# Stick-breaking attention of a prompt on one core: one-pass products for the logits, and merged suffix sums

## Chip, core and metric

The kernel runs on one core of a Trainium2 chip. The metric is the device time of one execution in microseconds (us). Engines are named as in the profile: PE is TensorE (matmuls), PEld its weight loads, DVE VectorE, ACT ScalarE, POOL GpSimd, SP SyncE, whose queue issues most DMAs. L2153 is line 2153 of the kernel before.

## The reference

One inference step of a two-layer decoder, for a prompt of 512 tokens and for 8 samples of 4 new tokens each, in f32. Layer 0 mixes tokens with a conformer convolution, layer 1 with stick-breaking attention (16 heads of 64 channels); each is followed by a gated FFN. What matters here is the attention of the prompt:

```python
z = jnp.einsum('bqhd,bkhd->bhqk', q, k) * (HEAD_DIM ** -0.5)
z = z + bias[None, :, None, None]
valid = k_pos[None, :] < q_pos[:, None]
log_fail = jnp.where(valid, jax.nn.log_sigmoid(-z), 0.0)
after = lax.cumsum(log_fail, axis=3, reverse=True) - log_fail
weights = jnp.where(valid, jnp.exp(jax.nn.log_sigmoid(z) + after), 0.0)
out = jnp.einsum('bhqk,bkhd->bqhd', weights, v)
```

For each query the weight of a key is a product of a sigmoid and of (1 - sigmoid) of all later keys before the query. With s = softplus(z) the logarithm of the weight is z minus the sum of s over this and all later keys. The samples attend to 256 cached tokens in pages of 128, and to their own new ones.

## The kernel before

**Arithmetic.** Most products are made of high and low parts. A value x is split into hi, x rounded to the type F32R, and lo = x - hi; a product is then three one-pass matmuls, hi with hi, hi with lo, lo with hi. A matmul with plain f32 operands takes the PE four passes, and shows in the trace as two instructions.

**Stages.** Layer 0, then in layer 1 the queries, then the keys (with the logits of the samples against the K pages in between), then one stage for the values, the attention of the prompt and the V pages of the samples, then the output projection, the FFN and the final norm. The change touches the third stage of layer 1, 746 to 919 us of the profiled execution.

**A planned stage.** Its instructions are not issued in program order. `Plan` (L75) collects operations, each with its engine, an estimated cost and what it reads and writes (`r`, `w`, and `a` for adding into a PSUM bank). `run` (L154) then gives each engine one fixed order by simulating these costs: of the operations that are ready it takes the one that can start first, with an advantage in proportion to its rank, the length of the longest chain behind it. On the chip each engine runs its order and waits on semaphores. `plan.tile` (L145) makes rings of buffers: a tile waits until the users of the one that many turns before are done.

**What the stage does.** For each chunk c of 128 channels, that is for each pair of heads, in this order of emission:

- `values` (L2024): V of the next chunk, as three-pass products (L2018 to L2020), and its transposition into `vtok` (L2046 to L2051), which goes to memory too.
- `page` (L2087): two of the 16 V pages of the samples. POOL gathers a page by an indirect DMA (L2094) into a ring of `PAGE_BUFS` = 3 buffers, PE multiplies it (L2105), and DVE or ACT adds the result into `oacc`.
- `pair` (L2142): the attention of the two heads j = 0 and 1, which lie on rows 0 to 63 and 64 to 127 of `qT` and `kT`.

`logits` (L2146) computes z transposed, keys on partitions and queries along the columns, so that a key chunk needs only the queries behind it. There are three groups of PSUM banks, two banks each: `zc` holds key chunk 3 against queries 384 to 511 (K3, 128 columns) and key chunk 2 against queries 256 to 511 (K2, 256 columns); `zb` holds key chunk 1 (384 columns); `za` key chunk 0 (512 columns). A bf16 product of the identity with `maskb2` then adds a large negative number where key and query conflict (L2156).

`softplus` (L2163) gives s in `spc`, `spb`, `spa` by exp, min, ln and max on ACT and DVE by turns. `parts_of` (L2172) makes the high part on POOL (`ha`, `hb`, `hc`) and the low part on DVE (`la`, `lb`, `lc`). `minus` (L2178) then subtracts suffix sums in PSUM by matmuls with constant weights: `ntri` is the triangle of -1 within a chunk, `nones` all -1 for whole later chunks; `ntri_r` and `nones_r` are the same in F32R. For `zc`, chunk 3 goes through f32 `ntri` and `nones` (L2205, L2206) and only chunk 2 and the sum of both chunks (columns 384 to 511 of `spc`, L2203) through parts. Last, ACT takes exp into `wc`, `wb` and `spa`, and `products` (L2231) multiplies the weights with `vtok`; the result replaces the queries in `qT` (L2240) and is split into `XH` and `XL` (L2261, L2262) for the output projection, whose first four groups (`begun`, L2266) belong to the same plan.

**Around it.** After the queries, `xT` (the residual) is saved to memory (L1716) and its place serves as page buffers `page_t` and for `wT`; L2257 loads it back on SP's queue before L2289 adds the output projection to it. `decode_weights` (L2061) turns the samples' logits `Zd`, `Zn` into weights `wT` and `wn` by a suffix sum of many DVE steps (L1891), at the start of the stage. `new_values` (L2119) adds the samples' own tokens into `oacc` and transposes it (L2132). The constants `nones`, `ntri`, `maskf`, `maskb` are made at the start of the kernel (L355 to L367), and their F32R and doubled forms at the start of the stage (L1974 to L1980).

Of the kernel before, what the change touches and what calls it, by code (L numbers as in the profile page):

```python
# [195 lines left out]
def tile_trunk(  # L196
# [84 lines left out]
    class Ring:  # L281
# [60 lines left out]
        def free(self, later=None):  # L342
# [16 lines left out]
    pool.affine_select(out=ntri, in_=ntri, compare_op=ALU.is_ge, fill=0.0, base=0,  # L359
                       pattern=[[-1, P]], channel_multiplier=1)  # L360
    maskf = base.tile([P, P], F32, name="maskf")
    pool.memset(maskf, 0.0)

    pool.affine_select(out=maskf, in_=maskf, compare_op=ALU.is_gt, fill=NEG, base=0,
                       pattern=[[1, P]], channel_multiplier=-1)
    maskb = base.tile([P, P], BF16, name="maskb")
    dve.tensor_copy(maskb, maskf)  # L367
    eps_t = base.tile([P, 1], F32, name="eps_t")
# [1402 lines left out]
    Zd = dz.tile([P, 4, KW], F32, name="Zd")  # L1771
    Zn = dz.tile([P, 4, NS], F32, name="Zn")
    Sn = dz.tile([P, 4, NS], F32, name="Sn")
    nsn = dz.tile([P, 4], F32, name="nsn")
# [192 lines left out]
    plan = Plan()  # L1967
    vw_cm, vw = open_pool("vw", side="right")
# [3 lines left out]
    wn = va.tile([P, 4, P], F32, name="wn")  # L1972
    oacc = vw.tile([P, 2, 2 * P], F32, name="oacc")
    nones_r = va.tile([P, P], F32R, name="nones_r")  # L1974
    dve.tensor_copy(nones_r, nones)
    ntri_r = va.tile([P, P], F32R, name="ntri_r")
    dve.tensor_copy(ntri_r, ntri)
    maskb2 = va.tile([P, 2, P], BF16, name="maskb2")
    for i in range(2):
        pool.tensor_copy(maskb2[:, i, :], maskb)  # L1980
    pool.memset(vtok_s, 0.0)
# [14 lines left out]
    def acost(n):  # L1996
        return 0.1 + n * 0.95e-3
# [144 lines left out]
    def pair(c):  # L2142
        zs = {}
        K3, K2 = (0, 3, 3 * P), (P, 2, 2 * P)

        def logits(tag, parts, mask):  # L2146

            z = zs[tag] = [psum(tag) for _ in range(2)]

            def f():  # L2150
                for i, (lo, kc, q0) in enumerate(parts):
                    for j in range(2):
                        pe.matmul(z[j]()[:, lo:lo + SEQ - q0], kT[HALF[j], c, kc * P:(kc + 1) * P], qT[HALF[j], c, q0:SEQ],  # L2153
                                  start=(i == 0), stop=False, skip_group_check=True)
                for j in range(2):
                    pe.matmul(z[j]()[:, 0:mask], identb, maskb2.rearrange("p i q -> p (i q)")[:, :mask],  # L2156
                              start=False, stop=True, skip_group_check=True)
# [24 lines left out]
        def sums(t):  # L2182
            return t.rearrange("p (a q) -> p a q", q=P)[:, 0:3:2, :]

# [7 lines left out]
        for j in range(2):  # L2192
            h = 2 * c + j
            b = bb[:, h:h + 1]
            spa, spb, spc = sbuf("spa", 512, 3), sbuf("spb", 384, 2), sbuf("spc", 512, 2)
            ha, hb, hc = sbuf("ha", 512, 1, F32R), sbuf("hb", 384, 2, F32R), sbuf("hc", 384, 2, F32R)
            la, lb, lc = sbuf("la", 512, 1, F32R), sbuf("lb", 384, 2, F32R), sbuf("lc", 384, 2, F32R)
            wb, wc = sbuf("wb", 384, 2), sbuf("wc", 384, 2)
            z3, z1, z0 = zc[j], zb[j], za[j]
# [10 lines left out]
            plan.op("act", acost(384), lambda wc=wc, z3=z3, b=b: act.activation(wc(), z3()[:, :384], AF.Exp, bias=b),  # L2210
                    r=[z3], w=[wc])
# [5 lines left out]
            plan.op("act", acost(384), lambda wb=wb, z1=z1, b=b: act.activation(wb(), z1()[:, :384], AF.Exp, bias=b),  # L2217
                    r=[z1], w=[wb])
            for x in (hb, lb):
# [8 lines left out]
            heads.append({3: (wc, slice(0, P)), 2: (wc, slice(P, 384)), 1: (wb, slice(0, 384)), 0: (spa, slice(0, 512))})  # L2228
        av = psum("one")
# [18 lines left out]
    for c in range(NC):  # L2248
# [7 lines left out]
        pair(c)  # L2256
    plan.op("sp", 3.0, lambda: nc.sync.dma_start(out=xflat, in_=xsave), w=["pages"] + [("wT", t) for t in range(4)])  # L2257
    plan.op("sp", 3.0, lambda: nc.sync.dma_start(out=vsv, in_=vtok_s[:NS, :]), r=[("vnew", i) for i in range(NC)])
# [22 lines left out]
    close(vw_cm)  # L2281
    close(vt_cm)
# [51 lines left out]
```

## Time and profile before

| | us |
|---|---|
| median of 3 runs | 1355.88 |
| lowest and highest | 1354.37, 1357.83 |
| the profiled execution, its own time | 1356.08 |
| span of its profile, first to last instruction | 1354.4 |
| stage of values and attention, within the span | 746 to 919 |

The profile's page gives busy time and share of the span for each engine, then the chain of work that ended last. A window row gives for one stretch the busy time of each engine, with the granted TensorE clock as a share of full speed. A timeline row has the start, the time until the last of the merged instructions ended, engine, line, operation, output and inputs, and their number; in brackets the idle time before it and what ended it. Matmuls overlap in the pipeline, so how long one takes is read from start to start. Grouped rows have the count, the busy time in us, the mean in ns and the idle time before.

### The profile page before, as it was taken

What the parts mean: (1) busy time and instruction counts of PE and PEld (TensorE: products, weight loads), DVE (VectorE), ACT (ScalarE), POOL (GpSimd) and SP (SyncE); (2) the same over time, 40 slices, a digit from 0 to 9 for tenths busy, and PEclk for the clock granted to TensorE, in tenths of its full rate; (3) what the DMA queues carried; (4) which work ended last, traced back from release to release, by engine and by line L of the source; (5) the groups of instructions that cost most, each with busy time, mean ns of one, the idle gap of its engine ahead of it and who ended that gap; (6) DMA issues with size and microseconds to landing.
All of it is one profiled execution on the core that took longest, in us unless ns stands there. A gap on an engine that the chain in (4) does not pass through costs nothing.

```text
span 1354.4 us, 26784 instructions
## 1 busy us (share of the span) xinstructions
PE 1318.0 (97%) x11018; PEld 1242.8 (92%) x11018; DVE 975.6 (72%) x1650; ACT 668.9 (49%) x1242; POOL 240.5 (18%) x379
## 2 busy tenths in 40 slices
PE   8999999999999999998999999999899999999997
PEld 7897799899999999998999777769899999999997
DVE  5599785878987877856253776663897896786762
ACT  6421574545554554544333566753654654454452
POOL 3201014301010010033221242222520010000012
PEclk9899999999999999999999999999999999999998
DMA  8273523123233233235365242322122233233221
GB/s 227 67 185 103 126 95 109 32 86 102 87 111 101 73 111 114 76 118 181 126 205 166 80 129 90 102 94 63 63 79 83 92 110 110 75 100 109 86 73 66
DMA packets 124492, 142.39 MB, mean 105 GB/s; under 512 B 5672, under 2 KB 117992, under 8 KB 124099
## 3 DMA queue, kind: packets, MB, share of 16 engines
q1 hardware_dynamic: 118003, 122.43, 29.4%
q0 software_dynamic: 6080, 18.25, 4.3%
q8 instruction: 86, 1.41, 0.4%
q14 instruction: 35, 0.29, 0.1%
q10 hardware_dynamic: 288, 0.02, 0.0%
HBM read 129.34 MB, written 12.18 MB: 104 GB/s over the span
## 4 chain that ended last, share of the span: by engine, by line
PE 84%; DVE 9%; ACT 3%; issue 1%; DMA 1%; POOL 0%; SPq 0%; DVEq 0%; ACTq 0%; POOLq 0%
PE acc L1441 5%; PE acc L1439 5%; PE acc L1440 5%; PE acc L425 4%; PE acc L426 4%; PE acc L427 4%; PE tr L1252 4%; PE tr L1251 4%; PE tr L1253 3%; PE av L1251 3%; PE av L1252 3%; PE av L1253 3%; PE acc L651 3%; PE acc L653 3%; PE acc L652 3%; PE tr L1441 3%
## 5 line engine op out<-in xcount | busy, mean ns | idle before, releaser
L328 DVE TENSOR_TENSOR wlo<-raw,whi 128x1024 fp32r<-128x1024 f32 (+2 forms) x244 | 258.5, 1064 | 77.5 <-ACT whi L325 77.1
L325 ACT CAST whi<-raw 128x1024 fp32r<-128x1024 f32 (+2 forms) x244 | 223.0, 916 | 153.5 <-PE tr L1252 30.5
L651 PE MATMUL acc<-XH,whi 128*128 128x288 f32 (+1 forms) x384 | 114.9, 299 | 0.0
L653 PE MATMUL acc<-XH,wlo 128*128 128x288 f32 (+1 forms) x384 | 111.0, 289 | 1.8 <-DVE wlo L328 1.8
L652 PE MATMUL acc<-XL,whi 128*128 128x288 f32 (+1 forms) x384 | 111.3, 290 | 0.0
L425 PE MATMUL acc<-XH,whi 128*128 128x288 f32 (+1 forms) x360 | 107.8, 300 | 0.6 <-DVE xT L1598 0.6
L426 PE MATMUL acc<-XL,whi 128*128 128x288 f32 (+1 forms) x360 | 104.0, 289 | 0.0
L427 PE MATMUL acc<-XH,wlo 128*128 128x288 f32 (+1 forms) x360 | 103.6, 288 | 0.0
L1441 PE MATMUL acc<-TH,wlo 128*128 128x272 f32 x288 | 83.4, 290 | 0.0
L1439 PE MATMUL acc<-TH,whi 128*128 128x272 f32 x288 | 83.2, 289 | 0.0
L1440 PE MATMUL acc<-TL,whi 128*128 128x272 f32 x288 | 83.1, 288 | 0.0
L1475 ACT COPY G<-acc 128x272 f32<-128x272 f32 (+1 forms) x72 | 26.9, 373 | 110.3 <-PE acc L1441 95.4
L651 PEld LDWEIGHTS acc<-XH,whi 128*128 128x128 f32 x384 | 72.7, 189 | 2.7 <-issue 2.1
L653 PEld LDWEIGHTS acc<-XH,wlo 128*128 128x128 f32 x384 | 72.8, 190 | 2.2 <-DVE wlo L328 2.2
L1252 PE MATMUL av<-HL,whi 128*128 128x288 f32 (+1 forms) x256 | 74.4, 290 | 0.0
L1251 PE MATMUL av<-HH,whi 128*128 128x288 f32 (+1 forms) x256 | 74.3, 290 | 0.0
L1253 PE MATMUL av<-HH,wlo 128*128 128x288 f32 (+1 forms) x256 | 74.0, 289 | 0.0
L1251 PE MATMUL tr<-HH,whi 128*128 128x256 f32 (+1 forms) x256 | 73.6, 288 | 0.0
L1252 PE MATMUL tr<-HL,whi 128*128 128x256 f32 (+1 forms) x256 | 73.4, 287 | 0.0
L652 PEld LDWEIGHTS acc<-XL,whi 128*128 128x128 f32 x384 | 72.8, 190 | 0.5
L1253 PE MATMUL tr<-HH,wlo 128*128 128x256 f32 (+1 forms) x256 | 73.0, 285 | 0.0
L1393 DVE SCALAR_TENSOR_TENSOR cv<-G,fprm,cv 128x560 f32<-128x560 f32 x88 | 69.9, 798 | 4.2 <-ACT cv L1390 3.0
(461 smaller groups left out, 4456.0 us busy)
## 6 DMA issues: line engine op xcount, KB each, us to landing
raw<-in_ffn_w_gate_dram SPq DMA_DIRECT2D x22, 1024.0 KB
raw<-in_ffn_w_up_dram SPq DMA_DIRECT2D x22, 1024.0 KB
raw<-in_ffn_w_down_dram SPq DMA_DIRECT2D x24, 768.0 KB
raw<-in_attn_w_qkv_dram SPq DMA_DIRECT2D x12, 1024.0 KB
raw<-in_conv_w_in_dram SPq DMA_DIRECT2D x6, 1024.0 KB
rep<-glu SPq DMA_DIRECT2D x36, 142.0 KB
raw<-in_conv_w_out_dram SPq DMA_DIRECT2D x4, 1024.0 KB
raw<-in_ffn_w_down_dram SPq DMA_DIRECT2D x8, 512.0 KB
```

Source lines behind the costliest of these rows:

```text
L325: act.copy(hi[:, :n, :], src)
L328: dve.tensor_tensor(lo[:, :n, :], src, hi[:, :n, :], op=ALU.subtract)
L425: pe.matmul(o, hi[:, k, :], xh[:, k, c0:c0 + n], start=(k == 0), stop=False)
L426: pe.matmul(o, hi[:, k, :], xl[:, k, c0:c0 + n], start=False, stop=False)
L427: pe.matmul(o, lo[:, k, :], xh[:, k, c0:c0 + n], start=False, stop=(k == nk - 1))
L651: pe.matmul(o, hi[:, k, :], XH[:, k, c0:c0 + n], start=(k == 0), stop=False)
L652: pe.matmul(o, hi[:, k, :], XL[:, k, c0:c0 + n], start=False, stop=False)
L653: pe.matmul(o, lo[:, k, :], XH[:, k, c0:c0 + n], start=False, stop=(k == NC - 1))
L1251: pe.matmul(o, hi[:, j + k, :], xh, start=(start and k == 0), stop=False, **kw)
L1252: pe.matmul(o, hi[:, j + k, :], xl, start=False, stop=False, **kw)
L1253: pe.matmul(o, lo[:, j + k, :], xh, start=False, stop=(stop and k == len(xs) - 1), **kw)
L1441: pe.matmul(o, lo[:, j + k, :], xh, start=False, stop=(k == 3), **kw)
```

## The change

Four things change.

1. **Logits.** Before a pair's logits, POOL copies the chunk of `qT` and of `kT` to F32R (`qh`, `kh`) and DVE subtracts (`ql`, `kl`), 512 columns each, in rings of one buffer. Each f32 product becomes three products of parts.
2. **Sums.** `hc` and `lc` are the parts of all 512 columns of `spc`. One `ntri_r` product of 384 columns for each part covers chunks 3 and 2, and one `nones_r` product of 128 columns takes chunk 3 off chunk 2; the f32 ones go.
3. **Weights in place.** The exponentials overwrite `spc` and `spb`, which become rings of three; `wc` and `wb` go.
4. **Places.** The constants are made on POOL after the queries, in the pools of the samples' attention. `Zn` and `Sn` move into the unused end of `xT`'s place. `wn` and `oacc` move into the third page buffer, so that V pages go through a ring of two, one page fewer is gathered ahead in the stage of the keys, and the reload of `xT` waits for `Zn`, `oacc` and `wn` as well.

```diff
-    nones = base.tile([P, P], F32, name="nones")
-    dve.memset(nones, -1.0)
-    ntri = base.tile([P, P], F32, name="ntri")
-    pool.memset(ntri, -1.0)
...
+    nones = small.tile([P, P], F32, name="nones")
+    pool.memset(nones, -1.0)
+    nones_r = dz.tile([P, P], F32R, name="nones_r")
+    pool.tensor_copy(nones_r, nones)
+    ntri_r = dz.tile([P, P], F32R, name="ntri_r")
+    pool.affine_select(out=nones, in_=nones, compare_op=ALU.is_ge, fill=0.0, base=0,
+                       pattern=[[-1, P]], channel_multiplier=1)
+    pool.tensor_copy(ntri_r, nones)
+    maskf = small.tile([P, P], F32, name="maskf")
+    pool.memset(maskf, 0.0)
+    pool.affine_select(out=maskf, in_=maskf, compare_op=ALU.is_gt, fill=NEG, base=0,
+                       pattern=[[1, P]], channel_multiplier=-1)
+    maskb2 = dz.tile([P, 2, P], BF16, name="maskb2")
+    for i in range(2):
+        pool.tensor_copy(maskb2[:, i, :], maskf)
...
-        if i >= 4 * NB:
+        if i >= 2 * NB + PAGE_BUFS - 1:
...
+    spare = page_t[(2 * NB - 1) % PAGE_BUFS]
+    wn = spare[:, 0:4 * P].rearrange("p (t r) -> p t r", t=4)
+    oacc = spare[:, 4 * P:].rearrange("p (g r) -> p g r", g=2)
...
-        t = plan.tile("page", PAGE_BUFS, lambda: page_t[(2 * NB + p) % PAGE_BUFS])
+        t = plan.tile("page", PAGE_BUFS - 1, lambda: page_t[(2 * NB + p % (PAGE_BUFS - 1)) % PAGE_BUFS])
...
+        qh, kh, ql, kl = (sbuf(tag, SEQ, 1, F32R) for tag in ("qh", "kh", "ql", "kl"))
+        for hi, x, lo in ((qh, qT, ql), (kh, kT, kl)):
+            plan.op("pool", 0.1 + SEQ * 1.2e-3, lambda hi=hi, x=x: pool.tensor_scalar(
+                hi(), x[:, c, 0:SEQ], 1.0, 0.0, op0=ALU.mult, op1=ALU.add), r=[("q", c)], w=[hi])
+            plan.op("dve", 0.6, lambda hi=hi, x=x, lo=lo: dve.tensor_tensor(
+                lo(), x[:, c, 0:SEQ], hi(), op=ALU.subtract), r=[("q", c), hi], w=[lo])
...
-                    for j in range(2):
-                        pe.matmul(z[j]()[:, lo:lo + SEQ - q0], kT[HALF[j], c, kc * P:(kc + 1) * P], qT[HALF[j], c, q0:SEQ],
-                                  start=(i == 0), stop=False, skip_group_check=True)
+                    for n_, (k, q) in enumerate(((kh(), qh()), (kh(), ql()), (kl(), qh()))):
+                        for j in range(2):
+                            pe.matmul(z[j]()[:, lo:lo + SEQ - q0], k[HALF[j], kc * P:(kc + 1) * P], q[HALF[j], q0:SEQ],
+                                      start=(i == n_ == 0), stop=False, skip_group_check=True)
...
-            plan.op("pe", 4 * n * COL + 0.4, f, r=[("q", c)], w=z)
+            plan.op("pe", 3 * n * COL + 0.2, f, r=[qh, kh, ql, kl], w=z)
...
-            minus(z3, lambda t: t[:, 0:P], ntri, spc, lambda t: t[:, 0:P], P, 2, [(spc, 0)])
-            minus(z3, lambda t: t[:, 256:384], nones, spc, lambda t: t[:, 0:P], P, 2, [(spc, 0)])
-            parts_of(hc, lc, lambda spc=spc: spc()[:, P:], 384, [(spc, 1), (spc, 2)])
+            parts_of(hc, lc, lambda spc=spc: spc(), 512, [(spc, 0), (spc, 1), (spc, 2)])
             for x in (hc, lc):
-                minus(z3, lambda t: t[:, P:384], ntri_r, x, lambda t: t[:, 0:256], 256)
+                minus(z3, lambda t: t[:, 0:384], ntri_r, x, lambda t: t[:, 0:384], 384)
+                minus(z3, lambda t: t[:, 256:384], nones_r, x, lambda t: t[:, 0:P], P)
...
-    plan.op("sp", 3.0, lambda: nc.sync.dma_start(out=xflat, in_=xsave), w=["pages"] + [("wT", t) for t in range(4)])
+    plan.op("sp", 3.0, lambda: nc.sync.dma_start(out=xflat, in_=xsave), w=["pages", "Zn"] + [("wT", t) for t in range(4)] +
+            [("oacc", bg) for bg in range(2)] + [("wn", t) for t in range(4)])
```

More of the change, by code (lines that the diff above doesn't have):

```diff
@@ L354, in tile_trunk @@
     dve.memset(mean_m, 1.0 / D)
-    nones = base.tile([P, P], F32, name="nones")
-    dve.memset(nones, -1.0)
-    ntri = base.tile([P, P], F32, name="ntri")
-    pool.memset(ntri, -1.0)
[L359 to L367, printed above, removed]
     eps_t = base.tile([P, 1], F32, name="eps_t")
@@ L1771, in tile_trunk @@
     Zd = dz.tile([P, 4, KW], F32, name="Zd")
-    Zn = dz.tile([P, 4, NS], F32, name="Zn")
-    Sn = dz.tile([P, 4, NS], F32, name="Sn")
+    Zn, Sn = (xflat[:, 4 * D + i * 4 * NS:4 * D + (i + 1) * 4 * NS].rearrange("p (t n) -> p t n", t=4) for i in range(2))
     nsn = dz.tile([P, 4], F32, name="nsn")
@@ L1967, in tile_trunk @@
     plan = Plan()
-    vw_cm, vw = open_pool("vw", side="right")
     va_cm, va = open_pool("va")
@@ L1971, in tile_trunk @@
     vtok_s = va.tile([P, D], F32, name="vtok_s")
[L1972 to L1980, printed above, removed]
+    spare = page_t[(2 * NB - 1) % PAGE_BUFS]
+    wn = spare[:, 0:4 * P].rearrange("p (t r) -> p t r", t=4)
+    oacc = spare[:, 4 * P:].rearrange("p (g r) -> p g r", g=2)
     pool.memset(vtok_s, 0.0)
@@ L2194, in pair @@
             b = bb[:, h:h + 1]
[L2195 to L2198, printed above, removed]
+            spa, spb, spc = sbuf("spa", 512, 3), sbuf("spb", 384, 3), sbuf("spc", 512, 3)
+            ha, hb, hc = sbuf("ha", 512, 1, F32R), sbuf("hb", 384, 2, F32R), sbuf("hc", 512, 2, F32R)
+            la, lb, lc = sbuf("la", 512, 1, F32R), sbuf("lb", 384, 2, F32R), sbuf("lc", 512, 2, F32R)
             z3, z1, z0 = zc[j], zb[j], za[j]
@@ L2204, in pair @@
                     r=[(spc, 0), (spc, 1)], w=[(spc, 2)])
[L2205 to L2207 removed]
+            parts_of(hc, lc, lambda spc=spc: spc(), 512, [(spc, 0), (spc, 1), (spc, 2)])
             for x in (hc, lc):
[L2209 to L2211 removed]
+                minus(z3, lambda t: t[:, 0:384], ntri_r, x, lambda t: t[:, 0:384], 384)
+                minus(z3, lambda t: t[:, 256:384], nones_r, x, lambda t: t[:, 0:P], P)
+            plan.op("act", acost(384), lambda spc=spc, z3=z3, b=b: act.activation(
+                spc()[:, :384], z3()[:, :384], AF.Exp, bias=b), r=[z3], w=[spc, *((spc, i) for i in range(3))])
             parts_of(hb, lb, lambda spb=spb: spb(), 384, [spb])
@@ L2216, in pair @@
                 minus(z1, lambda t: t[:, P:384], nones_r, x, sums, 256)
-            plan.op("act", acost(384), lambda wb=wb, z1=z1, b=b: act.activation(wb(), z1()[:, :384], AF.Exp, bias=b),
-                    r=[z1], w=[wb])
+            plan.op("act", acost(384), lambda spb=spb, z1=z1, b=b: act.activation(spb(), z1()[:, :384], AF.Exp, bias=b),
+                    r=[z1], w=[spb])
             for x in (hb, lb):
@@ L2227, in pair @@
                     r=[z0], w=[spa])
-            heads.append({3: (wc, slice(0, P)), 2: (wc, slice(P, 384)), 1: (wb, slice(0, 384)), 0: (spa, slice(0, 512))})
+            heads.append({3: (spc, slice(0, P)), 2: (spc, slice(P, 384)), 1: (spb, slice(0, 384)), 0: (spa, slice(0, 512))})
         av = psum("one")
```

3 lines of the change are left out of this document (1 added, 2 removed).

## The prediction

> **What bounds the kernel now.** I read the page's busy shares and chain first, then the stage of the prompt attention in windows, then inside it the matmuls, the weight loads, and what DVE and POOL do between them.
>
> ```profile
> PE 1318.0 (97%) x11018; PEld 1242.8 (92%) x11018; DVE 975.6 (72%) x1650; ACT 668.9 (49%) x1242; POOL 240.5 (18%) x379
> PE 84%; DVE 9%; ACT 3%; issue 1%; DMA 1%; POOL 0%; SPq 0%; DVEq 0%; ACTq 0%; POOLq 0%
> ```
>
> TensorE sets the whole. The change works in 746 to 919 us. In the windows each row is the stretch, its length, then busy time of PE, PEld, DVE, ACT, POOL, and the granted clock, DMA share, GB/s.
>
> ```profile
> 752.00:772.00 20.00, 18.94 (x151) 16.07 (x150) 18.41 (x45) 14.86 (x33) 5.87 (x8) 1.00 0.09 26
> 812.00:832.00 20.00, 20.00 (x169) 15.86 (x166) 12.14 (x25) 12.59 (x24) 5.94 (x8) 1.00 0.30 85
> 852.00:872.00 20.00, 20.00 (x162) 14.80 (x160) 13.77 (x28) 14.12 (x28) 6.42 (x8) 1.00 0.45 141
> 872.00:892.00 20.00, 18.73 (x130) 11.75 (x130) 15.37 (x30) 13.14 (x26) 4.65 (x7) 0.91 0.16 47
> 892.00:906.00 14.00, 12.87 (x132) 8.59 (x129) 11.70 (x25) 8.73 (x18) 3.55 (x6) 1.00 0.44 161
> 906.00:919.00 13.00, 13.00 (x106) 11.62 (x105) 2.65 (x6) 4.79 (x11) 0.03 (x1) 1.00 0.00 1
> ```
>
> Two things are to be seen. In the middle pairs PE is full (20.00 of 20), because products of values and pages fill the time in which a pair's softplus is on ACT and DVE: PE work taken away there can shorten the stage. In the first window DVE is nearly full (18.41), and in the last two pairs, where no values are left, PE has gaps (18.73 of 20, 12.87 of 14, and a clock of 0.91 in the first of them): there the DVE chain sets the pace, and added DVE work can lengthen it.
>
> **Logits.** One pair's three groups, each ended by its mask product:
>
> ```profile
> 852.72 1.13 PE L2153 MATMUL za<-qT,kT 64*128 64x512 f32 x4
> 853.79 0.28 PE L2156 MATMUL za<-maskb,identb 128*128 128x128 bf16 x2
> 854.00 1.08 PE L2235 MATMUL one<-spa,vtok 128*64 128x512 f32 x4
> ...
> 856.30 0.93 PE L2153 MATMUL zc<-qT,kT 64*128 64x128 f32 x8
> 857.16 0.39 PE L2156 MATMUL zc<-maskb,identb 128*128 128x256 bf16 x2
> 857.49 0.92 PE L2153 MATMUL zb<-qT,kT 64*128 64x384 f32 x4
> 858.33 0.28 PE L2156 MATMUL zb<-maskb,identb 128*128 128x128 bf16 x2
> ```
>
> Start to start: za 1.07, zc 0.86, zb 0.84, together 2.77 us. An f32 product is two instructions for each of two heads, and the two heads' halves (64 rows each) go side by side. From zb to za 128 more columns cost 0.23, over four passes 0.45 ns a column and pass; 4 x 512 of these at the 0.42 that follow below are 0.86, so some 0.2 us of each group is fixed. One-pass products stand in the sums:
>
> ```profile
> 794.00 0.38 PE L2179 MATMUL zc<-spc,ntri 128*128 128x128 f32 x2
> 794.21 0.39 PE L2179 MATMUL zc<-spc,nones 128*128 128x128 f32 x2
> 794.36 0.42 PE L2179 MATMUL zb<-hb,ntri_r 128*128 128x384 f32 x1
> 794.62 0.34 PE L2179 MATMUL zb<-lb,ntri_r 128*128 128x384 f32 x1
> 794.79 0.28 PE L2179 MATMUL zc<-hc,ntri_r 128*128 128x256 f32 x1
> 794.91 0.28 PE L2179 MATMUL zc<-lc,ntri_r 128*128 128x256 f32 x1
> ```
>
> A 384-wide one takes 0.17 (794.62 to 794.79), a 256-wide one 0.12: some 0.42 ns a column and a little, so 0.22 for 512. No row shows a one-pass product of 128 columns. Each product loads its own weight, and the loads give a floor:
>
> ```profile
> L2153 PEld LDWEIGHTS zc<-qT,kT x64: 182/188/189, 755.7 to 894.2; 64*128 64x128 f32 x64
> L2235 PEld LDWEIGHTS one<-spa,vtok x32: 132/134/137, 776.4 to 909.0; 128*64 128x64 f32 x32
> L2105 PEld LDWEIGHTS one<-xT x256: 105/110/178, 770.5 to 896.9; 128*32 128x32 f32 x128
> ```
>
> 128, 64 and 32 columns of f32 weights load in 188, 134 and 110 ns: 54 ns for 64 columns, so 0.11 us of streaming for 128, and a narrow product comes once in 0.11 and not in the 0.07 of its own columns. After the change: za 0.2 + 3 x 0.22 = 0.86, zb 0.2 + 3 x 0.17 = 0.71, zc 0.2 + 3 x 0.12 + 3 x 0.11 = 0.89. Together 2.46, 0.31 less; for 8 pairs **-2.5 us**: three passes instead of four, but each with a load of its own, and nothing for zc. Bounds for the narrow product: 0.07 (8 x 3 x 0.04 = 1.0 more saved, -3.5), and the 0.22 that an f32 product of that width takes (794.00 to 794.21, +0.1). I take 0.11, the nearest row.
>
> By the Trainium skill (TensorE: Matmul & The Clock Gate, section "Wait — 56ns, not 53.3ns?") back-to-back products of 128 columns start 55.6 ns apart; if that held for these, the logits and sums would save 3.1 us more (24 + 32 narrow products, each 0.055 shorter). The measured loads speak against it, and the sum leaves it out.
>
> **Sums.** From 794.00 to 794.62 the two f32 products and one 384-wide one take 0.62; less 0.17 they cost 0.45, with the two 256-wide ones 0.69 a head. Instead come two 384-wide ones (0.34) and two narrow ones (0.22): 0.56, 0.13 less, for 16 heads **-2.1 us** (with narrow ones of 0.07 -3.4, of 0.22 +1.4). PE in all: **-4.6**, between -6.9 and +1.5.
>
> **High and low parts.** Each pair adds two POOL copies and two DVE subtractions 512 wide, and each head's hc and lc grow from 384 to 512.
>
> ```profile
> L2175 DVE TENSOR_TENSOR la<-spa,ha 128x512 fp32r<-128x512 f32 x16 | 11.2, 700 | 2.8 <-POOL ha L2173 2.8
> L2175 DVE TENSOR_TENSOR lc<-spc,hc 128x384 fp32r<-128x384 f32 x16 | 10.9, 679 | 0.0
> L2173 POOL TENSOR_SCALAR ha<-spa 128x512 fp32r<-128x512 f32 x16 | 11.3, 705 | 84.3 <-DVE spa L2169 75.8 <-PE za L2179 5.1 <-DVE la L2175 3.1
> L2173 POOL TENSOR_SCALAR hc<-spc 128x384 fp32r<-128x384 f32 x16 | 10.9, 678 | 2.6 <-DVE spc L2203 2.6
> ...
> 884.36 0.87 DVE L2175 TENSOR_TENSOR lb<-spb,hb 128x384 fp32r<-128x384 f32 x1
> ...
> 885.93 0.68 DVE L2175 TENSOR_TENSOR la<-spa,ha 128x512 fp32r<-128x512 f32 x1
> ...
> 886.92 0.54 DVE L2175 TENSOR_TENSOR lb<-spb,hb 128x384 fp32r<-128x384 f32 x1
> ...
> 888.81 0.48 DVE L2114 SCALAR_TENSOR_TENSOR oacc<-one,own,oacc 128x256 f32<-128x256 f32 x1 [0.87 <-PE one L2105]
> ```
>
> DVE: 16 x 0.70 = 11.2 us, and lc grows by 0.54 to 0.68, 16 x 0.14 = 2.2: 13.4 in all, 1.68 a pair. POOL: 16 x 0.70 = 11.3 and up to 2; it has room (84.3 us idle ahead of ha alone). The parts of pair c+1 can be made as soon as pair c's three logits are through, some 15 us before they are wanted, and DVE is idle 6 us in 20 in the middle windows, such as the 0.87 at the end of a pair's chain: I cost 16 x 0.70 at nothing. What hides it is that idle time between a pair's last subtraction and the next pair's first exponential; without it, it costs up to 1.4 us a pair. The wider lc lies in the dense part of DVE; in the two last pairs, where PE waits for DVE, I count it, 4 heads x 0.14 = **+0.6** (0 to 2.2).
>
> The same subtraction took 0.87 with POOL busy beside it and 0.54 without. The Trainium skill has a rule that speaks against the change here (SBUF — State Buffer, on the shared port pair: a DVE operation with two SBUF inputs and a GpSimd one that reads SBUF exclude each other, and the loser waits out the whole instruction); the trace agrees (0.87 against 0.54). By it 16 more POOL copies could hold DVE for 16 x 0.70 = 11.2 us more at worst.
>
> **What is moved.** The constants go from the start of the kernel and of this stage to POOL after the queries.
>
> ```profile
> 751.27 1.67 DVE L1975 CAST nones_r<-nones 128x128 fp32r<-128x128 f32 x1
> ...
> 751.45 0.95 POOL L1981 MEMSET vtok_s<- 128x1024 f32 x1
> ...
> 630.94 0.15 POOL L1725 IOTA t<- 128x32 int32 x1
> ...
> 638.07 0.18 DVE L1765 CAST idx<-pt_f 128x16 int32<-128x16 f32 x1
> ```
>
> Their eight small POOL operations come after the iota, when POOL's next work, the gather of pages, waits for idx until 638: 7 us of cover for eight times some 0.3 (hc's 0.678 is for three times their columns), 2.4: cost 0 (2.4 if the cover were gone). The two casts vanish from DVE, where it is dense: -1.7. In their place the first pair's parts (two copies on POOL behind its memset, two subtractions) stand ahead of the first logits, 2.8 us. PE has value products to do meanwhile. I take **0** (-1.7 to +2.8).
>
> The third page buffer becomes wn and oacc, so value pages go through two, and the reload of xT waits for the last transposition of oacc.
>
> ```profile
> 897.34 0.34 SPq L2257 DMA_DIRECT2D xT<-xsave  x1
> ...
> 905.90 0.38 PE L2132 MATMUL one<-ident,oacc 128*128 128x128 f32 x2
> ...
> 917.30 0.42 DVE L2289 TENSOR_TENSOR xT<-acc,xT 128x256 f32<-128x256 f32 x1 [2.56 <-PE acc L2020]
> ...
> DMA to landing us min/median/max: 4.3/4.6/6.0
> ```
>
> The reload went out at 897.3 and was over by 906 (the window behind has 1 GB/s), under 8.7 us. Issued at 906.3 it lands by 915.0, ahead of 917.3: hidden with 2 us to spare; SP has nothing queued behind it that PE needs sooner. 16 pages are read from 770.5 to 896.9, one in 8 us, so with two buffers a gather has some 16 us for its 4.6: 0. The exponentials now write over spc and spb in rings of three; the second head's softplus must wait for the products of the pair before, which stand ahead of the zc and zb logits already (854.00 against 856.30): 0.
>
> **Sum.** -4.6 + 0.6 = -4.0 on the profiled execution's 1356.08 us (span 1354.4 and 1.7 around it): **1352.1**, 3.8 under the median of 1355.88.
>
> **Rivals.** *DVE takes over.* The 1.68 us of new DVE work a pair fall into the dense stretch between exponentials and subtractions, and PE runs out of other products. For it: DVE 18.41 of 20 at the start, PE gaps at the end. Against it: 6 idle us in 20 in the middle. At all pairs it costs 13.4 - 4.6 = +8.8; it is slower by more than 0.3% (4.1 us; below that a measurement of this kernel can't tell it from no change) once 8.5 of the 13.4 us, five pairs, lie on the path. I put it at six: 10.1 - 4.6 = +5.5, **1361.5**.
>
> *The gaps close too.* With other costs the planned order changes; if pair 6 loses its PE gap (1.27 in 872 to 892) and its clock loss (0.09 x 20 = 1.8), -4.0 - 3.1: **1349.0**. For it: both are of one place. Against it: DVE, which PE waits for there, gets more work, not less.
>
> *Narrow one-pass products are as slow as f32 ones.* 16 x 2 x 0.11 + 8 x 3 x 0.11 = 6.1 more: +2.1, **1358.2**. No row excludes it. Then two thirds of the change does nothing for PE.
>
> *A transfer is late.* Reload or a page comes some 3 us too late twice: +2, **1358**; the spare times above speak against it.
>
> **Chances.** Forecast 0.47, its own range 1349.2 (all narrow products at 0.07 and the casts' 1.7 not counted) to 1354.9 (the start's 2.8 lost); the bound of faster (1351.8) lies inside, 0.27 beyond it and 0.20 short of it. Gaps close 0.13. DVE takes over 0.27, slower. Narrow products 0.08, of which 0.05 within. Late transfer 0.05, slower. So faster 0.40, same 0.25, slower 0.35. The range goes from 1347.5 to 1362.0: it leaves out the upper part of the DVE case (some 0.12) and the ends of the others.
>
> **What would show it.** Logits: za's start to its mask 0.86 or less against 1.07, zc's unchanged near 0.89; narrow products 0.11 apart (0.07 or 0.22 decide that bound). Sums: four products in 0.56. DVE in 752 to 906 some 13 us busier, the new subtractions right behind a pair's last one; if they stand between exponentials and subtractions, or PE's idle time in the stage grows beyond what it now has, the DVE case holds. The stage from the first logits to the last page product shorter by 4 us, all other stages equal to 0.5. The forecast is wrong if PE's time in this stage does not fall, or falls and turns into waits.

## The result, and the profile after

The changed kernel takes **1365.64 us** in the median of five runs (1364.02 to 1368.79), the kernel before 1355.88: a ratio of 1.0077 (95% interval 1.0066 to 1.0088), so it is slower by about 10 us. The forecast was 1352.1. The profiled execution is the slowest of the five, 1368.79 us, with a span of 1367.1.

The page of the changed kernel, busy times and the shares of the chain that ended last:

```profile
PE 1318.4 (96%) x11050; PEld 1247.6 (91%) x11050; DVE 981.4 (72%) x1662; ACT 669.2 (49%) x1242; POOL 261.7 (19%) x397
PE 82%; DVE 10%; issue 2%; DMA 2%; ACT 1%; SPq 1%; POOL 1%; DVEq 0%; ACTq 0%; POOLq 0%
```

TensorE is as busy as before (1318.4 against 1318.0) in a longer span. The windows of its changed stage (the columns are those of the prediction):

```profile
784.00:804.00 20.00, 17.44 (x151) 13.53 (x151) 14.03 (x27) 9.70 (x20) 8.90 (x10) 1.00 0.44 144
824.00:844.00 20.00, 19.03 (x164) 15.06 (x165) 13.62 (x27) 12.08 (x25) 8.66 (x10) 1.00 0.24 69
864.00:884.00 20.00, 19.03 (x163) 15.13 (x163) 15.70 (x31) 14.77 (x30) 8.66 (x10) 1.00 0.23 73
884.00:904.00 20.00, 17.19 (x131) 11.95 (x131) 14.94 (x30) 12.15 (x25) 8.65 (x10) 0.91 0.39 123
```

The middle pairs, which had 20.00 of 20 on PE, now have 19.03. DVE and POOL are far from full there, so what is late is not a full engine but a wait. The timeline of one pair's logits on TensorE (start, length, instruction):

```profile
824.02 0.50 PE L2158 MATMUL za<-qh,kh 64*128 64x512 f32 x2
824.36 0.39 PE L2158 MATMUL za<-ql,kh 64*128 64x512 f32 x2
824.58 0.40 PE L2158 MATMUL za<-qh,kl 64*128 64x512 f32 x2
824.91 0.28 PE L2161 MATMUL za<-maskb,identb 128*128 128x128 bf16 x2
...
828.28 0.33 PE L2158 MATMUL zc<-qh,kh 64*128 64x128 f32 x2
828.44 0.28 PE L2158 MATMUL zc<-ql,kh 64*128 64x128 f32 x2
828.55 0.27 PE L2158 MATMUL zc<-qh,kl 64*128 64x128 f32 x2
...
829.17 0.39 PE L2161 MATMUL zc<-maskb,identb 128*128 128x256 bf16 x2
829.49 0.44 PE L2158 MATMUL zb<-qh,kh 64*128 64x384 f32 x2
...
830.21 0.29 PE L2161 MATMUL zb<-maskb,identb 128*128 128x128 bf16 x2
```

Start to mask: za 0.89 (forecast 0.86), zc 0.89 (0.89), zb 0.72 (0.71), in all 2.50 for 2.77, and the narrow products start 0.16 and then 0.11 apart (828.28, 828.44, 828.55), near the bound that the loads gave. So TensorE got the shorter work, and the time went elsewhere.

For this and every run below I cut each trace at three places: the first product of the values, the first product of weights and values of pair 0, and the same of pair 7. *Start* is the first stretch, *seven* the second (seven pairs), *idle* the sum, inside seven, of the gaps between the modelled end of a product and the start of the next, and *clock* half of the time inside seven that was granted at half speed. All in us, of the one profiled execution; what follows pair 7's products is 444.9 to 445.7 in all of them.

```
                     start   seven   idle   clock   ratio of times [95%]
before                29.7   132.6    3.0    1.7
changed               32.1   138.1   11.3    1.7    1.0077 [1.0066, 1.0088]
e1_f32_logits         29.7   131.6    6.2    0.0    1.0014 [1.0002, 1.0025]
e2_old_sums           31.0   145.4   13.9    5.1    1.0155 [1.0113, 1.0198]
e3_moves_only         32.7   131.4    3.2    1.7    1.0025 [1.0015, 1.0035]
e4_no_low_parts       30.8   139.7   11.1    3.4    1.0074 [1.0057, 1.0091]
e5_ksr_ahead          29.9   139.3   10.4    5.1    1.0055 [1.0037, 1.0074]
e7_two_buffers_no_low 30.3   140.4   10.3    5.1    1.0076 [1.0059, 1.0093]
e8_parts_once         31.8   139.9    9.7    5.1    1.0078 [1.0058, 1.0098]
e9_cost_of_before     35.2   136.1    9.5    1.7    1.0082 [1.0065, 1.0099]
e10_parts_once_cost4  33.5   131.8    6.3    1.7    1.0056 [1.0035, 1.0077]
e11_f32_cost3         29.7   140.3   10.1    3.4    1.0085 [1.0061, 1.0109]
e13_hb_on_act         31.8   134.5    7.9    1.7    1.0048 [1.0032, 1.0065]
e14_f32_hb_on_act     29.4   134.3    4.9    3.4    1.0030 [1.0018, 1.0042]
e15_order_of_four     33.5   136.9   11.4    0.0    1.0089 [1.0072, 1.0107]
e16_before_cost3      28.5   135.1    4.4    0.0    1.0013 [1.0003, 1.0023]
e17_hb_hc_on_act      31.4   154.4   16.6   15.4    1.0150 [1.0133, 1.0167]
e18_act_and_ksr       28.9   156.0   16.6   17.1    1.0191 [1.0174, 1.0208]
e19_act_same_order    31.9   130.7    6.1    0.0    1.0023 [1.0011, 1.0036]
e20_dve_same_order    32.7   138.1   11.4    1.7    1.0083 [1.0066, 1.0100]
```

From before to changed, seven grew by 5.5: TensorE's work fell by 2.8 (seven less idle, 129.6 to 126.8) and its idle time rose by 8.3. The start grew by 2.4. That is 7.9 of the 12.7 us between the two profiled executions. The rest lies ahead of the stage, where the trace of the changed kernel has 20.5 us at half clock and the trace of before has 6.8. e2, with nearly the same code there as the changed kernel, has 6.8 too, so this part is not put down to the change.

What TensorE waits for between 776 and 917 us in the changed kernel (in total, times, longest):

```profile
PE za L2184 <- POOL hc L2178: 5.6, 7, 1.8
PE za L2184 <- POOL hb L2178: 3.0, 2, 1.6
PE one L2101 <- DVE xT L2110: 2.4, 4, 0.8
```

The end of one pair's softplus on POOL, and then on DVE:

```profile
834.13 0.62 POOL L2178 TENSOR_SCALAR hc<-spc 128x512 fp32r<-128x512 f32 x1 [2.55 <-DVE spc L2207]
834.87 0.63 POOL L2178 TENSOR_SCALAR ha<-spa 128x512 fp32r<-128x512 f32 x1
835.46 0.52 POOL L2178 TENSOR_SCALAR hb<-spb 128x384 fp32r<-128x384 f32 x1
836.70 2.16 POOL L2178 TENSOR_SCALAR hb<-spb 128x384 fp32r<-128x384 f32 x1 [0.72 <-DVE spb L2174]
838.83 0.61 POOL L2178 TENSOR_SCALAR hc<-spc 128x512 fp32r<-128x512 f32 x1
```

```profile
835.15 0.61 DVE L2174 SCALAR_TENSOR_TENSOR spc<-zc,bb,spc 128x384 f32<-128x384 f32 x1
...
836.53 0.28 DVE L2207 TENSOR_TENSOR spc<-spc 128x128 f32<-128x128 f32 x1
836.73 0.68 DVE L2180 TENSOR_TENSOR lc<-spc,hc 128x512 fp32r<-128x512 f32 x1
837.33 0.55 DVE L2180 TENSOR_TENSOR lb<-spb,hb 128x384 fp32r<-128x384 f32 x1
837.80 0.68 DVE L2180 TENSOR_TENSOR la<-spa,ha 128x512 fp32r<-128x512 f32 x1
839.47 0.69 DVE L2180 TENSOR_TENSOR lc<-spc,hc 128x512 fp32r<-128x512 f32 x1 [0.99 <-POOL hc L2178]
840.08 0.48 DVE L2110 SCALAR_TENSOR_TENSOR xT<-one,own,xT 128x256 f32<-128x256 f32 x1
```

This is the place. The first hb takes 0.52. The second starts at 836.70, while DVE runs four operations with two SBUF inputs in a row, and ends 0.38 after the last of them (838.86 against 838.48): 2.16 us. Behind it on POOL stands the second hc, behind that on DVE the second lc, and behind lc in DVE's fixed order the addition of a V page's product into oacc (named xT here, in whose place it lies), for which TensorE waits too.

### The profile page after: what moved, and what is told of

Same layout as the page of the kernel before. It is cut to its first block, busy times and chain, and to the rows that moved or that the text cites. A ratio compares the mean times of both kernels' runs of the same rounds, so it can differ in the third digit from the quotient of the medians.

```text
span 1367.1 us, 26865 instructions
## 1 busy us (share of the span) xinstructions
PE 1318.4 (96%) x11050; PEld 1247.6 (91%) x11050; DVE 981.4 (72%) x1662; ACT 669.2 (49%) x1242; POOL 261.7 (19%) x397
## 4 chain that ended last, share of the span: by engine, by line
PE 82%; DVE 10%; issue 2%; DMA 2%; ACT 1%; SPq 1%; POOL 1%; DVEq 0%; ACTq 0%; POOLq 0%
PE acc L1428 5%; PE acc L1426 5%; PE acc L1427 5%; PE acc L412 4%; PE acc L413 4%; PE acc L414 4%; PE tr L1239 4%; PE tr L1238 3%; PE tr L1240 3%; PE av L1238 3%; PE av L1239 3%; PE av L1240 3%; PE acc L638 3%; PE acc L639 3%; PE acc L640 3%; PE tr L1428 3%
```

## The experiments

The chips of the sets differ a little, so I compare ratios to the kernel before on the same chip; 0.1% is 1.4 us.

**Which part costs it.** The first theory was that the parts of q and k cost it, above all as in the prediction's rival (DVE takes over with its new subtractions); against it stood the moves with the rings, and the wider hc of the merged sums. The first set undoes one part each.

e1, the logits f32 again and the q, k parts gone, the planner's cost with them:

```
-  for n_, (k, q) in enumerate(((kh(), qh()), (kh(), ql()), (kl(), qh()))):
+  pe.matmul(z[j]()[...], kT[HALF[j], c, ...], qT[HALF[j], c, q0:SEQ], ...)
-  plan.op("pe", 3 * n * COL + 0.2, f, r=[qh, kh, ql, kl], w=z)
+  plan.op("pe", 4 * n * COL + 0.4, f, r=[("q", c)], w=z)
```

> The changed kernel (1365.6 us) with the logits as before: f32 products straight from qT and kT, no high and low parts of them; merged sums, weights in place and all moves stay. Theory A (the parts of q and k are what costs: two POOL copies and two DVE subtractions a pair between exponentials and subtractions, and DVE blocked 2 us at the start behind a DMA): 1355 to 1358, PE's waits of over 0.25 us in the stage fall from 18.5 to under 11 us. Theory B (rings of three with weights in place, two page buffers, moved constants): 1363 to 1367. Theory C (wider hc and merged sums cost): 1363 to 1367 too.

e2, the sums of before (f32 ntri and nones, hc and lc 384 wide), the logits by parts:

```
-  parts_of(hc, lc, lambda spc=spc: spc(), 512, ...)
+  minus(z3, ..., ntri_f, spc, lambda t: t[:, 0:P], P, 2, [(spc, 0)])
+  minus(z3, ..., nones_f, spc, lambda t: t[:, 0:P], P, 2, [(spc, 0)])
+  parts_of(hc, lc, lambda spc=spc: spc()[:, P:], 384, ...)
```

> The changed kernel with the sums as before: f32 products with ntri and nones for key chunk 3, parts of 384 columns only; logits from parts, weights in place and all moves stay. Theory A: little changes, 1365 to 1368, since the merged sums save 2 us of PE. Theory B: the same. Theory C: hc of 512 columns comes after the sum of both chunks and PE waits for it at each pair, so without it 1358 to 1361.

e3, both edits together, so that only the moves, the rings and the shorter page ring stay:

> The changed kernel with logits and sums both as before: only the moved constants, the weights in place with rings of three, the two page buffers and the later reload are left. Theory A and C: the time of the kernel before, 1354 to 1358. Theory B: 1361 to 1366.

e4, the subtractions for ql and kl left out:

```
-  ... ((kh(), qh()), (kh(), ql()), (kl(), qh()))
+  ... ((kh(), qh()), (kh(), qh()), (kh(), qh()))
```

> The changed kernel without the low parts of q and k: the two DVE subtractions a pair are left out and the high parts stand in their place, so each logit is three times the product of the high parts; PE has the same products, POOL the same copies. Theory A, DVE's work as its cause: 1356 to 1360. If POOL's copies or the PE products are the cause: 1363 to 1366.

Measured: e1 1357.03, e2 1373.34, e3 1358.77, e4 1365.59 (before 1355.79). e2 lies above all that was expected of it, e3 just above the range for harmless moves. The moves cost 0.25%, in the profile all of it at the start (32.7 against 29.7). The merged sums pay: 0.11% from e3 to e1 (with intervals that overlap) and 0.78% from e2 to changed. The logits by parts cost 0.63% (e1 to changed) and 1.3% (e3 to e2). With 16 DVE subtractions fewer, e4 is where the changed kernel is: **DVE's new subtractions alone are not what makes it slow.**

**The start, and three theories.** What holds up the pairs could be POOL's queue with the new copies in it (theory B), the planned order (C) or the one-pass products themselves (D). And in the trace of the changed kernel the first pair's parts wait, on DVE:

```profile
755.02 0.69 DVE L2147 TENSOR_TENSOR ql<-qT,qh 128x512 fp32r<-128x512 f32 x1 [1.95 <-DMA out_dram<-ksr]
756.22 0.69 DVE L2147 TENSOR_TENSOR kl<-kT,kh 128x512 fp32r<-128x512 f32 x1 [0.51 <-POOL kh L2145]
```

The new ring lies over ksr, whose transfer out is still under way. e5 puts ksr elsewhere:

```
+    ksr = d1.tile([NS, D], F32, name="ksr")     (ahead of the tiles of the stage)
```

> The changed kernel with the tile ksr placed elsewhere, so that the first pair's ql no longer waits for ksr's outgoing transfer (2.0 us on DVE, 2.3 us on POOL in the profile of the changed kernel). If that wait is on the path, 1363.0 to 1364.0 (2 us less than 1365.64). If it is covered, 1365.0 to 1366.5. In both theories of the loop (POOL's queue, or the planned order) the period of 19.7 us a pair stays.

e7 is e4 with `qh, kh = (sbuf(tag, SEQ, 2, F32R) ...)`, two buffers for one, because POOL stands up to 11.4 us at qh for the logits that free it:

> The kernel without the low parts (1365.59; the subtractions for ql and kl left out, high parts used in their place) with qh and kh in rings of two instead of one. Theory B: what costs the 8 us is POOL's queue, where the copy qh waits up to 11.4 us for the last pair's logits to release the only buffer, with ha, hb and hc queued behind it: 1357 to 1361, and the wait of POOL at qh gone. Theory C: the planned order alone, or theory D, the products on TensorE: 1364.5 to 1366.5.

e8 makes the four parts once:

```
-  for hi, x, lo in ((qh, qT, ql), (kh, kT, kl)):
+  for hi, x, lo in ((qh, qT, ql), (kh, kT, kl)) if c == 0 else ():
```

> The changed kernel with the four parts qh, kh, ql, kl made for the first pair alone; the other seven pairs' logits use those (their own parts are left out, the products stay). Theory B (POOL's queue, or the POOL and DVE work of the parts as such): 1354 to 1358, at or under the 1357.0 with f32 logits, by up to the 2 us that TensorE's products are shorter. Theory D (the three one-pass products themselves cost it on TensorE): 1363 to 1366.

e9 changes one number, `3 * n * COL + 0.2` to `4 * n * COL + 0.4`:

> The changed kernel with the logits' cost in the planner put back to that of four passes (4 n COL + 0.4 instead of 3 n COL + 0.2); the work is the same, only the written-out order of the engines' queues can differ. Theory C (the planned order costs it): 1357 to 1361. Theories B and D: 1364 to 1367.

Measured: e5 1364.40, e7 1366.61, e8 1367.30, e9 1367.14 (before 1356.19). e5 came out between its two ranges, and its start is back at 29.9: the wait for ksr costs 2.2 us in the profile. In the other three the theory that each was made for did not come true. Leaving the parts' work out of seven pairs (e8) gains nothing, and so theory B as I had put it falls too: neither qh's wait nor the new copies by themselves are what makes it slow. C alone, as e9 puts it, gains nothing either. Two causes, each sufficient, were left as a possibility.

**Order against work.** e10 is e8 with e9's number. e11 is e1, whose logits really take four passes, with the planner told three: not one instruction differs from e1, only their order.

> The changed kernel with the four parts made for the first pair alone (the other pairs' own parts are left out) and the logits' planner cost put back to four passes: neither the parts' work nor the cost that the planner is told. Each alone left the time at 1367. If either of them was enough by itself, both gone give 1355 to 1358, at the 1357.0 of f32 logits or under it. If the one-pass products on TensorE, or how the queues are written out around them, cost it: 1363 to 1368.

> Merged sums and moves with f32 logits (1357.0), the logits' planner cost now that of three passes: the work is the same, only the order of the queues can differ. If the planned order is what costs it: 1362 to 1367. If the order is innocent: 1355.5 to 1358.5.

Measured: e10 1360.86, e11 1364.37 (before 1354.13). **e11 is the cleanest of all: the order alone takes seven from 131.6 to 140.3** and the ratio from 1.0014 to 1.0085. Of these 8.7 us 3.4 are half clock, which follows TensorE's waits (see the last section). In e10 seven is 131.8, as in e1; its start is late, and its time lies between its two ranges. So with neither the new order nor the new work the pairs are fast, and theory D falls. One line stands out on POOL, the group of hb copies from 776 us on (times | busy, mean ns | idle before). Before, then e1, then e11, then changed:

```profile
L2173 POOL TENSOR_SCALAR hb<-spb 128x384 fp32r<-128x384 f32 x14 | 7.5, 534 | 9.0 <-DVE spb L2169 8.9
```

```profile
L2170 POOL TENSOR_SCALAR hb<-spb 128x384 fp32r<-128x384 f32 x14 | 15.4, 1101 | 6.2 <-DVE spb L2166 6.2
```

```profile
L2170 POOL TENSOR_SCALAR hb<-spb 128x384 fp32r<-128x384 f32 x14 | 18.1, 1296 | 4.4 <-DVE spb L2166 4.4
```

```profile
L2178 POOL TENSOR_SCALAR hb<-spb 128x384 fp32r<-128x384 f32 x14 | 18.4, 1317 | 5.2 <-DVE spb L2174 5.2
```

The same copy of the same size takes 0.53, 1.10, 1.30 and 1.32 us. Most of this step is already in e1, which loses next to nothing, so a longer hb is not a loss by itself: it depends on who waits behind it. TensorE's longest waits from 776 to 917 us, in e1 and then in e11:

```profile
PE za L2176 <- POOL hb L2170: 4.2, 5, 1.5
PE za L2176 <- POOL hc L2170: 1.1, 3, 0.4
```

```profile
PE za L2176 <- POOL hc L2170: 5.0, 5, 1.2
PE za L2176 <- POOL hb L2170: 3.0, 2, 2.1
```

The order adds waits for hc above all. Theory E took up the copies: POOL's copies stand still behind DVE's subtractions, and the end of the pair behind them. e13 (from the changed kernel) and e14 (from e1) make hb on ACT:

```
-  plan.op("pool", 0.1 + m * 0.96e-3, lambda: pool.tensor_scalar(hi(), x(), 1.0, 0.0, ...), ...)
+  plan.op("act", acost(m), lambda: act.copy(hi(), x()), ...)     (for hb)
```

> The changed kernel with the high parts hb made on ACT instead of POOL. Theory E: POOL's second hb copy of a pair stands still while DVE's subtractions lc, lb, la run (2.16 us where the first copy takes 0.52), the second hc, which DVE and TensorE wait for, starts behind it, and this chain of the pair's end sets the period: 1.2 to 1.7 us less a pair, 1353 to 1359. If it is covered: 1363 to 1367.

> Merged sums and moves with f32 logits (1357.0), hb made on ACT. There POOL's hb also takes 1.10 us in the mean against 0.53 in the kernel before. Theory E: 0.5 us less a pair, 1351 to 1355. If it is covered: 1356 to 1359.

Measured: e13 1360.41, e14 1358.44. e13, between its two ranges, takes back 0.29 of the 0.77%; e14 missed (1.0030 for e1's 1.0014). In e13 hc became the copy that stands still (1302 ns in the mean), so the theory was neither shown nor refuted: every edit had also moved the order.

**Four more in orders of their own.** e15: planner's costs of four passes, and 0.01 for each of the parts. e16: the kernel before with `3 * n * COL + 0.2`. e17: e13 with hc on ACT as well. e18: e17 with e5's ksr.

> The changed kernel with the planner's costs as if the logits took four passes and the q, k parts nothing (0.01 each); the work is that of the changed kernel. If the planned order is the cause: 1356 to 1361. If the parts' own work in POOL's and DVE's queues holds the rest (as the 1367.1 with the cost of four alone suggests): 1364 to 1368.

> The kernel before with the planner's cost of the logits set to three passes, nothing else. If an order planned for shorter logits costs by itself, in any form of the sums: 1361 to 1367. If it needs the merged sums (whose first product of a pair waits for hc): 1354 to 1358.

> The changed kernel with the high parts hb and hc made on ACT; POOL keeps ha, qh and kh. If POOL's copies standing still behind DVE's subtractions are the rest of the loss: 1354 to 1359, under the 1360.4 with hb alone. If ACT's own queue becomes late, or the waits at the head of the pair (for the first hc) set the period: 1360 to 1366.

> The same as the run with hb and hc on ACT, and ksr placed elsewhere so that the first pair's parts don't wait for its transfer: 1.0 to 2.2 us under that run if the start's wait is on the path (the run with ksr alone was 1.2 us under the changed kernel), else within 0.8 us of it.

Measured: e15 1367.31, e16 1357.03, e17 1376.91, e18 1381.30 (before 1355.65). e16: in the kernel before the number costs little (1.0013; seven is 2.5 us longer, the start 1.2 shorter). So the order hurts far more in the changed kernel's form; whether the merged sums or the moves make it so was not told apart. e15: planned for four passes, the parts' work is what costs (136.9 against 131.8 in e10, where it is left out and the rest stands in nearly the same order); POOL's and DVE's shares of it were not separated. e17 and e18 went far the wrong way (e18's start is 2.5 us shorter than e17's, as meant, but its time is longer): TensorE waits for hc on ACT up to 1.7 us a time, and most of these waits bring a stretch of half clock (15.4 and 17.1 us in the column for it; see the last section). They say nothing on POOL, only that a copy moved off it can cost more than it frees.

**The same order, another engine.** The last two keep the changed kernel's order exactly: the planner is told POOL and its costs, and only the instruction is issued elsewhere.

```
-  plan.op("pool", 0.1 + m * 0.96e-3, lambda: pool.tensor_scalar(hi(), x(), ...), r=keys, w=[hi])
+  plan.op("pool", 0.1 + m * 0.96e-3, lambda: act.copy(hi(), x()) if on_act() else pool.tensor_scalar(...), ...)
```

In e19 `on_act` holds for both hb and for the second hc of a pair; e20 issues hb and hc on DVE instead.

> The changed kernel in its own planned order, with both hb and the second hc of a pair issued on ACT in place of POOL. In the changed kernel the second lc starts 2.8 us after the last spb (POOL's hb takes 2.16 us behind lc, lb and la, then hc 0.61). On ACT the two copies take about 1.1 us beside them, so the second lc can start about 1 us earlier. If the standing still sets the period: 0.6 to 1.2 us less a pair, 1356 to 1361. If it is covered by TensorE's other work and only the order counts: 1363.5 to 1367.

> The changed kernel in its own planned order (TensorE's, ACT's and SP's queues are the same), with hb and hc issued on DVE in place of POOL: DVE gets four copies more a pair, about 1.6 us at the 0.35 to 0.43 us of its other one-input operations of this size, and POOL none of them. If POOL's standing still sets the period: 1354 to 1360. If DVE's queue is what is late: 1368 to 1376. If neither is on the path: 1363.5 to 1367.

Measured: **e19 1358.40** (1.0023), e20 1366.02 (1.0083; before 1355.26). In e19 seven is 130.7 and idle 6.1, for 138.1 and 11.3 in the same order; 1.7 of the 7.4 us between them are half clock. The pair that was shown above, on ACT and then on DVE:

```profile
831.97 0.51 ACT L2184 CAST hb<-spb 128x384 fp32r<-128x384 f32 x1 [0.58 <-DVE spb L2180]
...
833.35 0.51 ACT L2184 CAST hb<-spb 128x384 fp32r<-128x384 f32 x1
833.77 0.62 ACT L2184 CAST hc<-spc 128x512 fp32r<-128x512 f32 x1
```

```profile
833.43 0.69 DVE L2186 TENSOR_TENSOR lc<-spc,hc 128x512 fp32r<-128x512 f32 x1
834.03 0.55 DVE L2186 TENSOR_TENSOR lb<-spb,hb 128x384 fp32r<-128x384 f32 x1
834.50 0.69 DVE L2186 TENSOR_TENSOR la<-spa,ha 128x512 fp32r<-128x512 f32 x1
835.10 0.69 DVE L2186 TENSOR_TENSOR lc<-spc,hc 128x512 fp32r<-128x512 f32 x1
835.78 0.48 DVE L2110 SCALAR_TENSOR_TENSOR xT<-one,own,xT 128x256 f32<-128x256 f32 x1
```

hb takes 0.51 beside the same three subtractions, and the second lc follows la at once: 1.67 us after the first lc's start, where it was 2.74 (836.73 to 839.47). TensorE's waits for hb and for xT are gone; the one for the first hc (5.5 us in e19, 5.6 in the changed kernel) is still there, so it isn't what this edit freed. e20 lies in the range for neither engine being on the path. Its waits read otherwise, as a gain and a loss of one size: its copies take 0.35 and 0.42 us on DVE, and the waits for hb and xT are nearly gone (0.2), but they lengthen the very queue that all wait for, and TensorE stands 7.6 us for hc and 3.2 for la and lb.

No kernel here beats the one before. e19 with e5's ksr might take the start's 2.2 us off as well; it wasn't run.

## Why the prediction was wrong

**Logits, -2.5 us: right.** 2.50 a pair for the forecast 2.46 and 2.77 before, -2.2 in eight pairs; the narrow products are 0.11 apart but for a first 0.16, near the bound I chose.

**Sums, -2.1: of this size, as far as the runs tell.** In the cleanest pair of runs, e3 and e1, the ratio falls by 0.11% (1.5 us), with intervals that overlap. TensorE's work in seven pairs fell by 2.8 in all, where -4.6 for eight gives -4.0; small stalls under a product's modelled end are inside that figure. Followed by another product of the sums, a narrow one takes 0.06 to 0.11 (starts at 823.65, 823.71 and 823.82 in the changed kernel), so there my 0.11 was the upper end.

**High and low parts, "I cost 16 x 0.70 at nothing": this step failed,** though not as its rival had it. The rival put 1.7 us of DVE work a pair into the dense stretch, 1361.5. Its direction was right, and a ql does stand in that stretch (at 832.24, ahead of the subtractions shown above), but without those subtractions the time is the same (e4). The step costed operations one by one in an order that it took as given. Three things were wrong in that. First, the change tells the planner a cheaper logits step, and this alone rewrites the order of all queues, for 8.7 us in seven pairs with no work changed (e11). I had this only as the rival in which gaps close. Second, even in an order planned for four passes the parts' work is not free: 5.1 us in seven pairs (e15 against e10). Third, I weighed POOL and DVE against each other in one direction, new POOL copies that hold up DVE. What happened is the other one: DVE's run of lc, lb and la holds up POOL's hb, and through it hc, lc and TensorE. Taking hb and the second hc off POOL in the unchanged order gives back 7.4 us of the seven pairs' time (e19), more than the 5.5 that they had lost. These figures overlap and are not terms of one sum. DVE itself became only 5.8 us busier in the whole, where I had 13: lb, which POOL had held up before, fell from 691 to 551 ns in the mean, lc stayed near 0.68 us though it got wider, and two casts of 3.2 us are gone.

The rule that I cited (the Trainium skill, SBUF — State Buffer, on the shared port pair) has both directions: whichever side starts first keeps the other out. This trace agrees, with 2.16 us for a copy of 0.52, and goes further: the rule has the lock for one instruction, and here POOL stayed out over a run of four. I applied it with the 0.87 of one subtraction and did not ask who waits behind a copy that is locked out.

**What is moved, 0 with bounds of -1.7 to +2.8: near the upper bound.** The start lost 2.4, as that bound said, but for a cause that I hadn't seen: the parts' tiles lie over ksr, and wait 2 us for its transfer (e5). With only the moves (e3) the start loses 3.0, 1.7 of it a half-clock stretch, and in e1, with the same moves, nothing; whether the difference is order was not tried. The reload went out 21 us later than before and was still hidden; SP's issue, and then the first DVE operation that needs its data:

```profile
918.89 0.34 SPq L2260 DMA_DIRECT2D xT<-xsave  x1
```

```profile
930.41 0.43 DVE L2292 TENSOR_TENSOR xT<-acc,xT 128x256 f32<-128x256 f32 x1 [2.58 <-PE acc L2016]
```

11.5 us lie between, and that operation waits for TensorE as it did before (2.58 and 2.56).

**What stays open.** Why the old sums with the new logits are the worst of the first set (e2, idle 13.9) I haven't taken apart, and how much of the order's cost is the first hc's wait rather than the copies that stand still was not told apart in e11. e19 moves hb and the second hc together, so their shares are not separated either.

## What to carry to other kernels

When the order of the queues is written by a planner, a change of one cost is a change of the whole order: try that number by itself, with the work left as it is, before putting a price on the work. When an edit adds to two engines of which one can keep the other out, look at which operations stand back to back on the one and who waits behind the other, not only at how full they are. To separate an engine's share from the order's, keep the plan and issue the instruction elsewhere.

## What the runs showed of the hardware

**A run of two-input operations on DVE can lock POOL out for its whole length.** hb took 0.52 while DVE ran operations that read one input from PSUM (the copy of 835.46, beside the operation of 835.15), and 2.16 beside four with two SBUF inputs, not just the length of one of them. In the twenty traces 52 hb copies met four such operations, and 50 of them ended 0.37 to 0.39 after the last. In e19 the same copies on ACT beside the same subtractions took 0.51 and 0.62 every time.

**POOL can win the same meeting.** In the kernel before, an hb that begins during the short addition into spc keeps its 0.51, and the subtraction behind that addition takes longer instead (the 0.87 at 884.36 in the prediction):

```profile
884.31 0.51 POOL L2173 TENSOR_SCALAR hb<-spb 128x384 fp32r<-128x384 f32 x1
```

```profile
884.15 0.28 DVE L2203 TENSOR_TENSOR spc<-spc 128x128 f32<-128x128 f32 x1
```

Of the meetings of this kind, with a subtraction next on DVE, POOL won 22 of 25 in the kernels with the old sums (before, e2, e3, e16) and 3 of 77 in those with the merged sums, whatever the order. Of the 25 won in all, POOL came straight from another copy in 18; of the 77 lost in all, it had stood idle ahead of 75. Whether that decides it, and whether the ports are kept from one operation to the next or won again each time, no run tells.

**A wait of TensorE is often paid twice.** Windows of e17, with the granted clock as the third number from the end:

```profile
832.80:836.20 3.40, 3.40 (x31) 3.15 (x32) 2.63 (x6) 3.40 (x9) 1.57 (x3) 1.00 0.78 267
836.20:839.60 3.40, 1.68 (x12) 1.15 (x10) 3.37 (x8) 2.19 (x5) 0.26 (x1) 1.00 0.00 0
839.60:846.40 6.80, 6.36 (x32) 5.09 (x32) 5.89 (x12) 2.50 (x5) 1.71 (x2) 0.50 0.35 87
```

A wait of 1.72 us for hc leaves TensorE busy for 1.68 of 3.4 us, and the next 6.8 run at half clock: up to 3.4 us more lost. In the twenty traces of this study there are 111 such stretches away from the kernel's end; 110 of them directly follow a window of 3.41 us in which TensorE was busy 65% of the time or less, and of 80 windows with 52% or less 70 were followed by one. The Trainium skill (TensorE: Matmul & The Clock Gate, Part 1) has the window of 3413 ns and the half clock after an idle one; here half an idle window was enough.
